# RWKV chunk loop of a two-layer trunk: scores called one stage earlier in the program, and score, mask and state tiles laid out for both directions or both heads at once

## The chip, the cores and the metric

One core of one Trainium2 chip runs the whole kernel. The metric is device microseconds (us) of one execution. Matrix products run on TensorE (PE in the profile; its weight loads are PEld), elementwise work on VectorE (DVE), ScalarE (ACT) and GpSimd (POOL), and DMAs are issued mostly by SyncE (SP).

## The reference, cut to what matters

The model is a trunk of two layers over 256 context and 1024 latent tokens. Each layer mixes tokens by three groups of heads and then runs a mixture of experts. The change concerns the first group, the RWKV-7 mixer: four heads of 64 channels, run over the 1280 tokens forward and backward.

```
def _rwkv7_step(state, inp):
    r, w, k, v, kk, a = inp
    sk = jnp.einsum('dbhvk,dbhk->dbhv', state, kk)
    state = state * w[..., None, :] - sk[..., :, None] * (kk * a)[..., None, :] + v[..., :, None] * k[..., None, :]
    return state, jnp.einsum('dbhvk,dbhk->dbhv', state, r)

def _rwkv7_mixer(za, za_c, lp, with_ctx):
...
    xs = (shared('r'), per_dir('w'), per_dir('k'), shared('v'), shared('kk'), per_dir('a'))
    s0 = jnp.zeros((2, Bn, A_HEADS, HEAD_DIM, HEAD_DIM), F32)
    _, ys = lax.scan(_rwkv7_step, s0, xs)
...
```

Here d is the direction, h the head. The decay w, the key k and the gate a differ by direction; r, v and kk are shared.

## The kernel before, in words

The scan is not run token by token. `rwkv` walks through ten stages of 128 tokens in each direction; a stage holds two chunks of 64 tokens (c), for two directions (d), two pairs of heads (hp) and two heads in a pair (e, one on partitions 0 to 63, the other on 64 to 127). So a stage has 16 units of 64 tokens. Per stage there are four parts.

- `front` (L719 to L790) loads r, k, kk and the low-rank activations, multiplies them out on PE (pu, L735), takes tanh, a running sum (cum, L746) and exponentials, and builds two sets of operands: L1 (kk and r times decays, L776 and L777, one head by DVE and the other by POOL) and bk (b and k times inverse decays, L784 and L785). bw is bk times the decay of the chunk.
- The scores (L798 to L844) turn bw round on PE (pb, L809) into L2 (L812, by ACT), and multiply bk with L1 (pa, L824, each product 128 rows of output: the wanted blocks and others). DVE masks pieces of the result into L1 (L829), Ly (L831) and low (L833); low of direction 0 has products of its own (pf, L840, masked at L841). L1, L2 and Ly are the matrices that the state is multiplied with; low is the strictly lower triangular matrix of a unit.
- The inverse of one plus low: low goes to DRAM and comes back with a 16 by 16 block on each partition (lan, then al). DVE inverts the blocks (`inv16`: L950, then 14 pairs L955 and L956, then L957), and they go back through DRAM into z16 and zt16 (tiles named z). Three products of 16 units and three DVE operations join them to blocks of 32 (`mm8`, L853, called at L857 to L859: pe, pzt, pz), two more sets join those to 64 (L864 and L873, with ACT in between). The result is tt.
- The chain (L889 to L940), two steps in each stage, one per chunk: px (L904) multiplies the state X with L1, ACT copies it (xy, L906), pu2 (L912) multiplies with tt, ACT and DVE write the negated result into X (L913 and L914), pm (L924 and L926) multiplies with Ly and L2, and DVE adds the parts: the new state nx (L930) and the output ys (L935), which a DMA stores per stage (L940). `new_pvu` (L708) makes the tile of the next state and has ACT copy the values v into it (L713). The next step's px needs nx, so the 20 steps of a layer are a chain.

Between these parts `more()` takes the next piece of `in_BC`, the input projection of the other heads: long runs of 16-bit products on PE (L528 to L530, L539 to L541), which depend on nothing in this loop.

The order of every engine's instructions is not the program's. A scheduler sets it when the kernel is built: of the instructions whose inputs its own timeline has ready, it takes the one that stands first in the program, and each engine then works through its queue in that order, waiting where a semaphore is not there yet. Tiles with a tag share `bufs` buffers, and PSUM tiles here come from pools of one to three banks (ps and psc two, psi one); an instruction that needs a buffer waits for its last reader. The first product of the loop starts 229 us into the span in layer 0 and 1997 us in layer 1.

## Time and profile before

| what | value |
|---|---|
| three runs, median (lowest to highest) | 3551.89 us (3545.98 to 3552.17) |
| profiled execution, its own time | 3544.36 us |
| span of the profiled execution | 3541.6 us |
| PE busy in the span | 2930.6 us (83%) |
| DVE busy | 2285.5 us (65%) |
| ACT busy | 1544.1 us (44%) |
| POOL busy | 1007.7 us (28%) |

The span is the time from the first to the last instruction; the execution takes 2.8 us more. Busy time of PE includes products that overlap in the array, so its share says how seldom PE stood still, not how well it was used. A wait is put down to the instruction that released it last. The names of buffers are given without their numbers: L stands for L1 and L2, z for z16 and zt16, pe for the first product of `mm8` and for the one at L864, pu for L735 and pu2 both.

### The profile page before, as it was taken

The page shows a single profiled execution, that of the slowest core. Times are in us where ns is not written, and L with a number is a line of the kernel's source. Part 1 is how long each engine was busy: PE and PEld are TensorE (multiplying, and loading weights), DVE is VectorE, ACT ScalarE, POOL GpSimd, SP SyncE. Part 2 cuts the span into 40 slices and gives each one's busy share as a digit, 9 for nine tenths or more (in the row PEclk, how much of TensorE's full clock was granted, in tenths as well). Part 3 has the DMA queues.
Part 4 walks back from the last instruction along what each step waited for, and adds up shares of the span by engine and source line. Part 5 has one row for each costly group of instructions (what it writes and reads, how often), then busy time and mean ns, then how long its engine had stood idle before and what let it go on. Part 6 is the DMA issues. An engine that isn't in the chain of part 4 may idle for free. (4 is left out here: it accounts for less than half of the span.)

```text
span 3541.6 us, 71217 instructions
## 1 busy us (share of the span) xinstructions
PE 2930.6 (83%) x28620; PEld 1833.0 (52%) x28620; DVE 2285.5 (65%) x4614; ACT 1544.1 (44%) x2769; POOL 1007.7 (28%) x998
## 2 busy tenths in 40 slices
PE   7998889989998788888737998898889866778864
PEld 4656567666755444443325565666666443334431
DVE  4356877368769454557678677783776845554775
ACT  4342444345643154456544434443565314343651
POOL 1122453134424211111165225331433321101113
PEclk9998889999999899999858988899899978888987
DMA  9764343282355789999862542433732769899995
GB/s 375 297 194 111 80 104 89 70 237 71 113 176 199 278 315 384 385 379 367 334 227 78 158 106 77 105 103 95 200 107 73 258 235 363 338 393 364 349 347 198
DMA packets 425468, 773.11 MB, mean 218 GB/s; under 512 B 211152, under 2 KB 340848, under 8 KB 394160
## 3 DMA queue, kind: packets, MB, share of 16 engines
q1 hardware_dynamic: 388048, 697.84, 56.7%
q0 software_dynamic: 36368, 68.07, 5.7%
q8 instruction: 227, 3.72, 0.4%
q10 hardware_dynamic: 720, 2.62, 0.3%
q14 instruction: 105, 0.86, 0.1%
HBM read 653.31 MB, written 114.97 MB: 217 GB/s over the span
## 5 line engine op out<-in xcount | busy, mean ns | idle before, releaser
L1664 PE MATMUL pgate<-wgp,hT 128*32 128x256 f16 (+2 forms) x1704 | 353.1, 376 | 101.8 <-ACT wgp L1613 60.8
L1664 PEld LDWEIGHTS <-hT 128*32 128x32 f16 (+2 forms) x3408 | 206.7, 108 | 334.0 <-issue 172.7
L529 PE MATMUL acc<-hL,wH 128*128 128x256 f16 (+2 forms) x1040 | 346.4, 334 | 13.4 <-POOL hL L486 13.4
L528 PE MATMUL acc<-hH,wH 128*128 128x256 f16 (+2 forms) x1040 | 345.6, 335 | 7.6 <-DVE hH L485 6.6
L530 PE MATMUL acc<-hH,wL 128*128 128x256 f16 (+2 forms) x1040 | 345.4, 333 | 0.0
L1704 PE MATMUL pd<-wdp,gT 128*32 128x256 f16 (+2 forms) x1704 | 221.1, 369 | 37.6 <-DVE gT L1691 21.6
L1195 POOL TENSOR_SCALAR s<-s,rd 128x640 f32<-128x640 f32 (+2 forms) x216 | 171.6, 794 | 222.3 <-DVE rd L1191 97.4
L1622 POOL DMA_INDIRECT xg<-hmoe,map x69 | 87.7, 1271 | 508.4 <-PE ptx L1628 454.5
L1664 PE MATMUL pgate<-wup,hT 128*32 128x256 f16 (+1 forms) x1224 | 196.9, 347 | 19.8 <-DVE wup L1614 12.7
L1614 DVE SCALAR_TENSOR_TENSOR wgp<-wg,wgp 128x2048 f16<-128x2048 f32 x74 | 166.4, 2287 | 63.2 <-ACT wgp L1613 63.1
L1614 DVE SCALAR_TENSOR_TENSOR wdp<-wd,wdp 128x2048 f16<-128x2048 f32 x74 | 166.5, 2287 | 46.9 <-ACT wdp L1613 46.9
L1184 ACT ACTIVATE s<-s,nm 128x640 f32<-128x640 f32 (+2 forms) x216 | 164.4, 763 | 66.1 <-DVE nm L1181 48.6
L1614 DVE SCALAR_TENSOR_TENSOR wup<-wu,wup 128x2048 f16<-128x2048 f32 x74 | 166.3, 2286 | 30.0 <-ACT wup L1613 27.7
L1208 PE MATMUL po<-pt,vt 128*64 128x128 f32 x1920 | 166.9, 288 | 20.2 <-DVE pt L1199 11.7
L1293 PE MATMUL acco<-wo,o 128*128 128x512 f16 x756 | 177.2, 388 | 0.0
L1704 PEld LDWEIGHTS <-gT 128*32 128x32 f16 (+2 forms) x1704 | 97.0, 108 | 147.4 <-DVE gT L1691 30.0
L1613 ACT ACTIVATE wdp<-wd 128x2048 f16<-128x2048 f32 x74 | 137.2, 1903 | 51.0 <-DMA wd<-w_down 44.1
L1717 POOL DMA_DIRECT2D ys<-y x66 | 51.7, 784 | 378.5 <-DVE y L1711 206.9
L1613 ACT ACTIVATE wup<-wu 128x2048 f16<-128x2048 f32 x74 | 137.3, 1903 | 48.7 <-DMA wu<-w_up 48.7
L1613 ACT ACTIVATE wgp<-wg 128x2048 f16<-128x2048 f32 x74 | 137.4, 1902 | 46.0 <-DMA wg<-w_gate 42.7
L1165 PE MATMUL pss<-k,qs 128*128 128x256 f16 (+1 forms) x552 | 127.5, 269 | 31.9 <-DVE mx L1178 18.4
L1672 ACT ACTIVATE sg<-pgate 64x512 f32<-64x512 f32 (+2 forms) x86 | 42.8, 498 | 251.9 <-PE pgate L1664 251.9
(420 smaller groups left out, 7424.2 us busy)
## 6 DMA issues: line engine op xcount, KB each, us to landing
wu<-w_up SPq DMA_DIRECT2D x64, 2048.0 KB
wd<-w_down SPq DMA_DIRECT2D x64, 2048.0 KB
wg<-w_gate SPq DMA_DIRECT2D x64, 2048.0 KB
wmod<-w_mod SPq DMA_DIRECT2D x48, 1024.0 KB
w<-w_in SPq DMA_DIRECT2D x41, 512.0 KB
ld<-ys SPq DMA_DIRECT2D x40, 384.0 KB
z<-inv SPq DMA_DIRECT2D x80, 128.0 KB
ys<-y POOLq DMA_DIRECT2D x20, 512.0 KB
```

The source lines that it names most:

```text
L528: self.nc.tensor.matmul(ov, H[:, k, :], hh, start=k == 0, stop=False)
L529: self.nc.tensor.matmul(ov, H[:, k, :], hl, start=False, stop=False)
L530: self.nc.tensor.matmul(ov, Lo[:, k, :], hh, start=False, stop=k == KD - 1)
L1165: te.matmul(pss[:, o:o + n], qs[:, e, Q], k1[:, e, k0:k0 + n], start=True, stop=False)
L1184: a.activation(s2[:, e, :nk], s2[:, e, :nk], AF.Exp, bias=nm[:, e:e + 1], scale=1.0 / SS, accum_out=den[:, e:e + 1])
L1195: g.tensor_scalar(s2[:, e, :nk], s2[:, e, :nk], rd[:, e:e + 1], SC_Q, OP.mult, OP.mult)
L1208: te.matmul(po[64 * e:64 * e + 64, 0:P], vt[:, kb, 64 * e:64 * e + 64], pt[:, e, x * P:x * P + P], start=x == 0, stop=x == len(kbs) - 1)
L1293: te.matmul(acc, o[:, zo, k] if k < KD - 1 else self.og_last[:, zo, tok], wo[:, zw, k, c], start=k == 0 and y == 0, stop=k == KD - 1 and y ...
L1613: nc.scalar.mul(t[:, 0, c], w[:, c], SC_W)
L1614: nc.vector.scalar_tensor_tensor(t[:, 1, c], w[:, c], SC_W, t[:, 0, c], OP.mult, OP.subtract)
L1664: te.matmul(p[off + i * m:off + i * m + m, :n], part(hT, zh)[:, k, o:o + m], part(w, zw)[:, k, i * n:i * n + n], start=k == 0 and y == 0, ...
L1704: te.matmul(t, part(gT, zh)[:, k, :m], part(wd, zw)[:, k, i * n:i * n + n], start=k == 0 and y == 0, stop=k == 3 and y == len(parts) - 1)
```

## The change

In the program's text the stage is taken apart: a new function `scores(st, ahead)` holds the scores and `inv16`, and it is called for stage st+1 before the joining of the blocks and the chain of stage st; `front` is called for stage st+2 there. Around this, tiles get another order of their dimensions so that one instruction covers what several did:

- L1's operands are made by four DVE operations (one per head and operand, both directions and all chunks) in place of four on DVE and four on POOL.
- The product of all 128 rows (pa) becomes three sets of 64 by 64 blocks: pk (the other head's rows, 128 columns), pr and pf for both directions. DVE masks four pk pieces, one pr and one pf per stage, where it had four, four, and three.
- The running sum takes both pairs of heads at once, `new_pvu` both directions, the copy to L2 both directions, and ys is one operation per step, stored per step.
- `mm8` leaves out the columns that are zero or unchanged: 32 columns in place of 64, and a standing tile E4 with zeros takes the place of E.
- b and k keep the places that they have in bk.

The core of the diff:

```
+            nc.sync.dma_start(vt[st][:, :, 0], self.vst[:, 2 * FSEG[st]:2 * FSEG[st] + 2])
+            for s in range(2):
+                nc.sync.dma_start(vt[st][:, s, 1], self.vst[:, 2 * BSEG[st] + 1 - s])
...
             for d in range(2):
-                for hp in range(2):
-                    v.tensor_tensor_scan(cum[:, d, hp], k2("scan"), th[:, d, hp], 0.0, OP.mult, OP.add)
+                v.tensor_tensor_scan(cum[:, d].rearrange("p h t -> p (h t)"), k2("scan"), th[:, d].rearrange("p h t -> p (h t)"), 0.0, OP.mult, OP.add)
...
-            for d in range(2):
-                for e in range(2):
-                    eng = v if e == 0 else g
-                    eng.tensor_tensor(L1v[hom[e], d, :, e, e], chv(kk_)[hom[e], d], chv(ex)[hom[e], d], OP.mult)
-                    eng.tensor_tensor(L1v[hom[e], d, :, e, 1 - e], chv(r_)[hom[e], d], chv(cum)[hom[e], d], OP.mult)
...
+            for e in range(2):
+                o = hom[e]
+                for i, (x, y) in enumerate(((kk_, ex), (r_, cum))):
+                    v.tensor_tensor(L1p[o, :, :, e, i], pieces(x)[o], pieces(y)[o], OP.mult)
...
+        def scores(st, ahead):
             L1, bk, bw, wt, seg = ahead
-            if st < 9:
-                ahead = front(st + 1)
-            more()
...
-                            te.matmul(pas[e][:, i * 128:i * 128 + 128], bk[hom[e], d, hp, c].rearrange("p s t -> p (s t)"),
-                                      L1[hom[e], d, c, hp, e].rearrange("p s t -> p (s t)"), start=True, stop=True)
...
+                            te.matmul(pk[hom[1 - e], 2 * hp + c], bk[hom[e], d, hp, c, 1 - e, :],
+                                      L1[hom[e], d, hp, c, e].rearrange("p s t -> p (s t)"), start=True, stop=True)
+                for e in range(2):
+                    o = hom[1 - e]
+                    v.tensor_tensor(L1[o, d, :, :, e].rearrange("p h c s t -> p (h c) (s t)"), pk[o],
+                                    k2(f"mL1_{d}")[o].unsqueeze(1).to_broadcast([64, 4, 128]), OP.mult)
...
+                            te.matmul(pr[hom[e], i], b_, r1, start=True, stop=True)
+
+                            x, y = (K_, b_) if d == 0 else (b_, K_)
+                            te.matmul(pf[hom[e], i], x, y, start=True, stop=True)
+            v.tensor_tensor(Ly.rearrange("p d h c t -> p d (h c) t"), pr.rearrange("p (d u) t -> p d u t", d=2),
+                            k2("mR").rearrange("p (d t) -> p d t", d=2).unsqueeze(2).to_broadcast([P, 2, 4, 64]), OP.mult)
+            v.tensor_tensor(low.rearrange("p d h c t -> p (d h c) t"), pf, k2("mLow").unsqueeze(1).to_broadcast([P, 8, 64]), OP.mult)
...
             z16, zt16 = self.inv16(rp, st % 2)
+            return L1, L2, Ly, lowu, z16, zt16, wt, seg
+
+        ahead = front(0)
+        made = scores(0, ahead)
+        ahead = front(1)
+        for st in range(10):
+            L1, L2, Ly, lowu, z16, zt16, wt, seg = made
+            if st < 9:
+                made = scores(st + 1, ahead)
+            if st < 8:
+                ahead = front(st + 2)
+            more()
...
-            E = rp.tile([P, 8, 64], F32, tag="E", name="E", bufs=1)
-            v.tensor_tensor(E, mm8("pe4", lowu, zt16), k2("mE4").unsqueeze(1).to_broadcast([P, 8, 64]), OP.mult)
-            v.tensor_tensor(zt16, zt16, mm8("pzt", z16, E), OP.subtract)
-            v.tensor_tensor(z16, z16, mm8("pz", E, z16), OP.subtract)
...
+            lo16, up16 = halves(z16)[:, :, :, 0], halves(zt16)[:, :, :, 1]
+            Eh = halves(E4)[:, :, :, 1]
+            v.tensor_tensor(Eh, mm8("pe4", lowu, up16), k2("mE4").rearrange("p (g t) -> p g t", t=16).unsqueeze(1).to_broadcast([P, 8, 2, 16]), OP.mult)
+            pzt = mm8("pzt", z16, Eh)
+            v.tensor_tensor(up16, up16, pzt, OP.subtract)
+            v.tensor_tensor(lo16, lo16, mm8("pz", E4, lo16), OP.subtract)
...
-                for e in range(2):
-                    o = hom[1 - e]
-                    for d in range(2):
-                        c = s if d == 0 else 1 - s
-                        v.tensor_tensor(ys[o, d, c], pm[o, 1, d], xy[o, d, :, e, :], OP.add)
+                ys = rp.tile([P, 2, 2, 64], F32, tag="ys", name="ys", bufs=2)
+                v.tensor_tensor(ys, pm[:, 1], xy[:, 1], OP.add)
+                for d in range(2):
+                    nc.sync.dma_start(y_d[d, 2 * seg[d] + cs[d]], ys[:, d])
```

The scheduler makes another order of it. Three places follow; the line numbers in the rows of the changed kernel are its own.

**PE, layer 0, around the first step of a chain.** In the kernel before, at a place where px of one stage stands (L904, its operand is L_3014):

```order
L904 MATMUL px<-pvu,L_3014 64x64 x16
L853 MATMUL pe_4361<-z_1_4357,low 64x64 x16
L840 MATMUL pf<-bk,L_4167 64x64 x6
L912 MATMUL pu_4033<-xy,z_1_3847 64x64 x4
L912 MATMUL pu_4033<-xy,z_0_3843 64x64 x4
L840 MATMUL pf<-bk,L_4167 64x64 x2
```

In the changed kernel, where px has the operand L_2172 (L924 is px, L931 pu2, L871 `mm8`, L822 pk, L836 pr, L839 pf):

```order
L944 MATMUL pmy<-pvu,L_2185 64x64 x8
L942 MATMUL pmy<-pvu,Ly 64x64 x8
L822 MATMUL pk<-L_3425,bk 64x128 x16
L871 MATMUL pe_4045<-z_1_3375,low 64x32 x7
L924 MATMUL px<-pvu,L_2172 64x64
L871 MATMUL pe_4045<-z_1_3375,low 64x32
L924 MATMUL px<-pvu,L_2172 64x64 x15
L871 MATMUL pe_4045<-z_1_3375,low 64x32 x2
L836 MATMUL pr<-L_3425,bk 64x64 x15
L839 MATMUL pf<-bk,L_3425 64x64 x5
L931 MATMUL pu_3723<-xy,z_1_2306 64x64 x4
L931 MATMUL pu_3723<-xy,z_0_2302 64x64 x4
```

In both, the first product of the next stage's joining (pe) and the scores of the stage after it (L_4167, L_3425) stand around px of the chain's stage; what moved is that pk, pr and pf now follow one another in that place, where pa stood in pieces among other work.

**DVE, layer 0, around the start of an inverse.** Before (L914 writes X, L930 the next state, L950 starts the inverse):

```order
L829 TENSOR_TENSOR L_3657<-pa,c_1919 64x2x2x128
L831 TENSOR_TENSOR Ly<-pa,c_1919 64x2x2x64
L833 TENSOR_TENSOR low<-pa,c_1919 64x256
L914 TENSOR_SCALAR pvu<-pu_3534 64x2x2x64
L841 TENSOR_TENSOR low<-pf,c_1919 128x256
L930 TENSOR_TENSOR pvu<-pmy,xw 64x2x2x64 x2
L935 TENSOR_TENSOR ys<-pmy,xy 64x128 x4
L950 TENSOR_TENSOR zl<-c_1919,al 64x256
```

In the changed kernel (L933 writes X, L948 the next state, L876 and L878 belong to `mm8`, L965 starts the inverse):

```order
L826 TENSOR_TENSOR L_2356<-pk,c_1919 64x4x128 x4
L933 TENSOR_SCALAR pvu<-pu_3048 64x4x64
L840 TENSOR_TENSOR Ly<-pr,c_1919 128x512
L842 TENSOR_TENSOR low<-pf,c_1919 128x512
L876 TENSOR_TENSOR E_1939<-pe_3543,c_1919 128x16x16
L1085 TENSOR_TENSOR xp<-prope,rope 128x512
L948 TENSOR_TENSOR pvu<-pmy,xw 64x4x64 x2
L950 TENSOR_TENSOR ys<-pmy,xy 128x256
L965 TENSOR_TENSOR zl<-c_1919,al 64x256
L970 TENSOR_TENSOR il<-al,zl 64x14
L971 TENSOR_TENSOR zl<-zl,il 64x14
L878 TENSOR_TENSOR z_1_2306<-z_1_2306,pzt 128x16x16
```

The operation that finishes the joined block zt16 (L878) now stands behind the start of the next stage's inverse.

**DVE, layer 0, around the end of an inverse.** Before, at the end of one inverse (L957 is its last operation):

```order
L955 TENSOR_TENSOR il<-al,zl 64x26
L914 TENSOR_SCALAR pvu<-pu_3972 64x2x2x64
L956 TENSOR_TENSOR zl<-zl,il 64x2x13
L955 TENSOR_TENSOR il<-al,zl 64x14
L956 TENSOR_TENSOR zl<-zl,il 64x14
L957 COPY zl<-zl 64x256
```

In the changed kernel (L972 is the last operation of the inverse):

```order
L970 TENSOR_TENSOR il<-al,zl 64x26
L971 TENSOR_TENSOR zl<-zl,il 64x2x13
L970 TENSOR_TENSOR il<-al,zl 64x14
L971 TENSOR_TENSOR zl<-zl,il 64x14
L972 COPY zl<-zl 64x256
L933 TENSOR_SCALAR pvu<-pu_3664 64x4x64
L506 SCALAR_TENSOR_TENSOR wL<-w,wH 128x1024
L948 TENSOR_TENSOR pvu<-pmy,xw 64x4x64 x2
```

The operation that writes X for the first step of the stage (L933) moved from among the inverse's last operations to behind them.

## Rows read from the trace of the kernel before

**Rows 1.** Stretches by engine: us, busy per engine, granted clock, DMA share and GB/s.

```profile
core 0: us, PE busy (x) PEld busy (x) DVE busy (x) ACT busy (x) POOL busy (x), PEclk, DMA share, GB/s
...
348.00:704.00 356.00, 315.33 (x4571) 226.20 (x4568) 240.00 (x595) 140.12 (x360) 131.47 (x129) 0.90 0.34 88
400.00:500.00 100.00, 87.24 (x1114) 59.50 (x1113) 77.79 (x173) 41.81 (x108) 53.30 (x49) 0.85 0.37 95
500.00:600.00 100.00, 87.42 (x1311) 66.43 (x1309) 79.28 (x206) 43.45 (x116) 40.69 (x39) 0.93 0.38 94
...
2113.00:2462.00 349.00, 315.63 (x4653) 229.02 (x4652) 240.68 (x594) 140.83 (x359) 129.80 (x124) 0.92 0.34 87
```

**Rows 2.** DVE's X product, both layers: form, count | busy, mean ns | idle before, releaser.

```profile
L914 DVE TENSOR_SCALAR pvu<-pu 64x256 f32<-64x256 f32 x40 | 17.1, 427 | 67.1 <-ACT pvu L913 66.5
```

**Rows 3.** DVE in layer 0, start us and us: from low to the inverse.

```profile
529.42 0.42 DVE L841 TENSOR_TENSOR low<-pf,c 128x256 f32<-128x256 f32 x1
531.82 0.87 DVE L930 TENSOR_TENSOR pvu<-pmy,xw 64x256 f32<-64x256 f32 x2 [1.98 <-PE pmy L924]
532.62 0.99 DVE L935 TENSOR_TENSOR ys<-pmy,xy 64x128 f32<-64x128 f32 x4
...
537.38 0.42 DVE L950 TENSOR_TENSOR zl<-c,al 64x256 f32<-64x256 f32 x1 [3.18 <-issue]
```

**Rows 4.** SP in the same stretch: the load of the blocks.

```profile
534.16 0.59 SPq L947 DMA_DIRECT2D al<-lan  x1
```

**Rows 5.** DVE groups of both layers, by form, as in rows 2.

```profile
L829 DVE TENSOR_TENSOR L<-pa,c 64x512 f32<-64x512 f32 x80 | 54.8, 684 | 11.1 <-PE pa L824 10.2
L784 DVE SCALAR_TENSOR_TENSOR bk<-th,wv 64x512 f32<-64x512 f32 x40 | 46.1, 1152 | 1.3 <-ACT wv L756 0.7
L777 DVE TENSOR_TENSOR L<-ld,cum 64x256 f32<-64x256 f32 x40 | 42.5, 1095 | 0.2
L935 DVE TENSOR_TENSOR ys<-pmy,xy 64x128 f32<-64x128 f32 x160 | 39.0, 283 | 8.0 <-PE pmy L924 7.5
L776 DVE TENSOR_TENSOR L<-ld,ex 64x256 f32<-64x256 f32 x40 | 35.4, 918 | 0.7 <-ACT ex L757 0.5
L746 DVE TENSOR_TENSOR_SCAN cum<-c,th 128x128 f32<-128x128 f32 x80 | 34.9, 485 | 0.6
L831 DVE TENSOR_TENSOR Ly<-pa,c 64x256 f32<-64x256 f32 x80 | 33.8, 422 | 1.2
L833 DVE TENSOR_TENSOR low<-pa,c 64x256 f32<-64x256 f32 x40 | 16.6, 414 | 1.4 <-PE pe L864 1.3
L857 DVE TENSOR_TENSOR E<-pe,c 128x512 f32<-128x512 f32 x20 | 13.7, 685 | 9.1 <-PE pe L853 8.7
L955 DVE TENSOR_TENSOR il<-al,zl 64x56 f32<-64x56 f32 x40 | 10.7, 267 | 1.1
L841 DVE TENSOR_TENSOR low<-pf,c 128x256 f32<-128x256 f32 x20 | 8.4, 420 | 10.6 <-PE pf L840 10.2
```

**Rows 6.** PE groups of both layers, by form.

```profile
L824 PE MATMUL pa<-L,bk 64*128 64x128 f32 x640 | 80.5, 310 | 12.0 <-DVE zl L956 5.2 <-DVE Ly L831 4.2 <-ACT L L812 2.4
L853 PE MATMUL pe<-z,low 64*64 64x64 f32 x640 | 32.4, 243 | 22.5 <-DMA z<-inv 22.5
```

**Rows 7.** PE in layer 1: runs of like products, start us, us of the run, rows.

```profile
2383.02 0.32 PE L875 MATMUL p<-z,E 32*32 32x32 f32 x10
2383.28 1.16 PE L824 MATMUL pa<-L,bk 64*128 64x128 f32 x8
...
2384.92 0.93 PE L824 MATMUL pa<-L,bk 64*128 64x128 f32 x6
...
2418.93 0.38 PE L529 MATMUL acc<-hL,wH 128*128 128x512 f16 x1
2419.24 0.33 PE L853 MATMUL pe<-z,low 64*64 64x64 f32 x2
2419.49 0.39 PE L530 MATMUL acc<-hH,wL 128*128 128x512 f16 x1
2419.81 0.92 PE L853 MATMUL pe<-z,low 64*64 64x64 f32 x24
...
2420.92 0.33 PE L853 MATMUL pe<-z,low 64*64 64x64 f32 x4
```

More of the change, by code (lines that the diff above doesn't have):

```diff
@@ L790, in front @@
             return L1, bk, bw, wt, seg
-        ahead = front(0)
-        for st in range(10):
+        def scores(st, ahead):
             L1, bk, bw, wt, seg = ahead
-            if st < 9:
-                ahead = front(st + 1)
-            more()
             low = rp.tile([P, 2, 2, 2, 64], F32, tag="low", name="low", bufs=2)
@@ L810, in rwkv @@
             for e, pb in enumerate(pbs):
[L811 to L815 removed]
+                a.copy(L2[:, :, :, :, e].rearrange("p d h c t -> p (d h c) t"), pb.rearrange("p (u t) -> p u t", t=64))
             for d in range(2):
[L819 removed]
+                pk = ps.tile([P, 4, 128], F32, tag=tag, name="pk")
@@ L835, in rwkv @@
-            pf = ps.tile([P, 512], F32, tag=tag, name="pf")
-            for hp in range(2):
-                for c in range(2):
-                    for e in range(2):
-                        i = 2 * hp + c
-                        te.matmul(pf[hom[e], i * 64:i * 64 + 64], L1[hom[e], 0, c, hp, e, e, :], bk[hom[e], 0, hp, c, e, :], start=True, stop=True)
-            v.tensor_tensor(low[:, 0], pf[:, 0:256].rearrange("p (h c t) -> p h c t", h=2, c=2), mask("mLow", slice(0, 128), 64), OP.mult)
+                            te.matmul(pk[hom[1 - e], 2 * hp + c], bk[hom[e], d, hp, c, 1 - e, :],
+                                      L1[hom[e], d, hp, c, e].rearrange("p s t -> p (s t)"), start=True, stop=True)
@@ L938, in rwkv @@
             more()
-            for d in range(2):
-                nc.sync.dma_start(y_d[d, 2 * seg[d]:2 * seg[d] + 2].rearrange("c p h t -> p c h t"), ys[:, d])
     def inv16(self, rp, b):
```

89 lines of the change are left out of this document (42 added, 47 removed).

## The prediction

> **What bounds the kernel now.** I first read the stretches by engine [rows 1]. The loop runs from 348 to 704 us in layer 0 (ten stages, 35.6 us each) and from 2113 to 2462 in layer 1 (34.9 each). No engine is full: DVE is busy for 240 us of 356, PE for 315. But in the middle stages (400 to 600) PE stands at 87% and DVE at 78 to 79%, at a granted clock of 0.85 to 0.93. Two engines near full, each waiting for the other in turn, is what the reader should see.
>
> Next, the groups by line, to find where the chain waits. DVE is idle for 67.1 us before the X product (L914), and 66.5 of these end with ACT's half of the same pair [rows 2]: ACT had waited for pu2, and pu2 for tt. So the chain is late because the inverse's tail is late, in the first of a stage's two steps. The inverse is late for a reason that DVE's timeline shows: low is finished at 529.84, but the inversion begins at 537.38, 7.5 us later [rows 3]. In between DVE does chain work (nx 0.87, ys 0.99) and waits 3.18 us; SP issues the load of the blocks at 534.16 [rows 4], so the way through DRAM is what it waits for. The ring is: L1's operands, scores and masks on DVE, DRAM, 28 small operations of DVE, DRAM, joining on PE and DVE, X, the next state. Most of its links are on DVE, in one queue.
>
> **Look-ahead.** By the text the scores come one stage earlier. By the order of the queues they hardly do: in both kernels, while the chain of a stage runs, the next stage is being joined and the one after is scored (the operands in the rows of PE's order). I cost this part at zero; the change is worth the work that it takes off DVE and PE.
>
> **DVE, both layers (20 stages)** [rows 5].
> Removed: L776 35.4 and L777 42.5, the scan 34.9, Ly 33.8, low 16.6 and 8.4, three operations of `mm8` per stage (60 at 0.685, as E, 41.1), ys 39.0. Together 251.7.
> Added:
> - 80 operations for L1 of 64x512, without a row of their own. The nearest of this size are the pa mask with one input in PSUM (0.684) and bk with both in SBUF (1.152). I take the middle, 0.92: 73.6 (54.7 to 92.2).
> - 40 scans of 256 elements: 0.485 for 128, so at most 0.97; by the slope between 256 and 512 elements elsewhere (0.422 and 0.684, 1.02 ns each) 0.62. I take 0.75: 30 (24.6 to 38.8).
> - Ly and low over all 128 partitions at 0.684, 20 each: 27.4.
> - 60 operations of `mm8` with 256 elements at 0.42 (as L841): 25.2. 40 ys at 0.42: 16.8.
> Together 173.0, a saving of 79 us (51 to 103), 3.95 per stage. The four pk masks per stage have the size of the four pa masks: no change.
>
> The rows speak for the dear end of the first price: L777, both inputs in SBUF and POOL at work beside it, takes 1.095 for half of that size, where L831 with an input in PSUM takes 0.422. The Trainium skill (SBUF — State Buffer, section "Who interferes with whom") says that DVE's second pair of ports is shared with GpSimd as an exclusive lock; by it the new operations would be slow wherever POOL works beside them, and the saving would be some 60, an estimate. The trace agrees that these forms are slow; POOL itself loses its half of L776 and L777, so the lock would be held less.
>
> **PE, both layers.** pa is 640 rows in the trace; two more rows in a run cost 1.16 − 0.93 = 0.23, so 0.115 each [rows 7]: 73.6. pk has as many, each of 64 by 128, and its two heads sit in opposite quarters of the array. Products of 64 columns that sit so (L853) cost (0.92 − 0.33)/20 = 0.0295 a row [rows 7] (two to 24 rows of one line); for 128 columns that is 0.059: 37.8. If they don't overlap, 73.6. pf's 320 rows become 1280 of pr and pf: 960 more at 0.0295, +28.3. `mm8`'s 1920 rows go from 0.0295 to between that and half of it, I take 0.017: −24. The order has about 100 fewer changes between kinds of product, at some 0.1 each (a lone pair takes 0.33 [rows 7], against 0.06 in a run): −10. Net −41.5, from −51 to about 0, or 2.1 per stage.
>
> The order puts pk's two heads into one bank of PSUM. L853 does the same with its two halves, and 24 rows still take 0.92 us [rows 7], so I count the overlap. The Trainium skill (TensorEngine Tiling (Array Packing), section "Gotcha 1: PSUM Pressure") says that different row tiles cannot access the same bank at once; by it pk would keep 0.115 a row and PE would save about 6 us, an estimate. The trace here disagrees for L853's products.
>
> **At nothing.** ACT issues fewer copies (v, L2) and POOL loses its half of the operands; neither is waited for with more than a few us. SP gets three more DMAs per stage (v and y), 0.59 each as the row of SP has it [rows 4], 1.8 us per stage; the cover is that SP's queue has no work of its own, and if it went, al's issue would be late by that. The input projection left over behind the chain gets 48 products of 512 columns shorter in layer 0 and 48 longer in layer 1, at 0.38 [rows 7] 18 us each way: zero.
>
> **The sum.** I take DVE's saving as the stage's, for its queue holds most of the ring; PE's (31.5 a stage less 2.1, in a stage of 31.3 to 31.6) is then covered by it, and becomes next in line. The last two stages of each layer make no new front or inverse, so 16 stages count: 16 × 3.95 = −63 us. The profiled execution took 3544.4 (span 3541.6 and 2.8 around it), the runs' median is 7.5 above. On the median's scale: 3552 − 63 = **3489**; by DVE's ends (51 and 103, eight tenths of each) 3470 to 3511. What is late next is PE.
>
> **Rivals.**
> 1. PE alone sets the time: only PE's saving counts and its idle time stays. For it: PE's 87% in the middle [rows 1]. Against: the 67 us [rows 2] are a wait for the ring, not for PE's queue. 3552 − 41 = 3511.
> 2. Both count, and the wait of the first joining product for z's landing (22.5 us [rows 6]) goes, because the inverse is done earlier. −63 − 41 − 22 = 3425. For it: the order has the inverse's end well ahead of pe. Against: PE can't be more than full.
> 3. Slower: head-of-line waits on DVE. In the new order the inversion's start (L965) stands before L878, and the X product of the first step (L933) behind the whole inverse. Between low and L965 there is now less chain work (0.42 and 0.87 and 0.42, 1.7 us), so of the 7.5 us up to 5.8 are a wait instead of 3.2: +2.6. And X may have to let 22 operations of the inverse at 0.267 and four L1 operands at 0.92 pass, 9.6 us, against some 26 products of PE at 0.243 [rows 6] (6.3) that lie before pm anyway: +3.3. Less the 3.95 saved: +1.9 × 16 = +31, 3583. It decides from the point at which PE reaches pm before DVE has ended the inverse. For it: the order. Against: the scheduler's timeline thought all of these ready by then, and SP's issue of al comes soon after low.
> 4. The change does not do what it says: look-ahead was there, and DVE's freed time becomes a longer wait for al (3.18 of 7.5 already is [rows 3]). 3552.
>
> **How the numbers follow.** The forecast gets 0.41: it rests on the one wait that is long and on rows for most of its terms. PE alone 0.17, both 0.14, slower 0.18, nothing 0.10. Faster by over 0.2% (7 us, about what a measurement of this kernel can tell from no change) is 0.41 + 0.17 + 0.14 = 0.72; same 0.10; slower 0.18. The range leaves out half of rival 2 below 3425 and most of rival 3 above 3560: 3425 to 3560. The forecast's own range is 3470 to 3511.
>
> **What would show it.** In the changed profile: stages of about 31.3 us; the L1 operands (L790) at 0.7 to 1.15, Ly and low (L840, L842) near 0.68, ys (L950) at 0.42; DVE busy about 40 us less in each layer; the 67 us before the X product (now L933) down to a third. For PE: a run of pk at 0.06 a row; at 0.115 the overlap failed. For rival 3: idle time before L965 above 3.2 a stage, and idle PE before pm released by DVE's X. For rival 4: stages of 35 us with DVE idle more. The prediction is wrong if DVE's work falls as counted and the stage stays above 34 us, or if PE's busy share in the middle stages goes to 95% with DVE idle.

## The result, and the profile after

The change made the kernel slower: 3596.97 us (median of four runs, 3591.78 to 3600.37) against 3548.93 for the kernel before on the same chip, a ratio of 1.0138 with a 95% interval of 1.0114 to 1.0162. The forecast was 3489, with a range from 3425 to 3560. The profiled execution has a span of 3592.3 us, 50.7 more than before.

Where it went. In layer 0 nothing was lost: the last state of the chain comes at 707 us (688 before), but the products of the input projection that are left over behind the chain end at 730 (734 before). In layer 1 the last state comes at 2482 (2453), and the left-over products end at 2525 (2467), so 58 us are lost there. The stretches show why; they are the changed kernel's, by engine, with the columns of [rows 1]:

```profile
348.00:704.00 356.00, 309.60 (x4867) 230.49 (x4866) 225.44 (x493) 131.76 (x312) 109.79 (x97) 0.91 0.35 87
2113.00:2462.00 349.00, 278.77 (x4248) 205.99 (x4246) 224.46 (x478) 119.44 (x278) 104.24 (x89) 0.84 0.33 82
2462.00:2520.00 58.00, 58.00 (x854) 43.30 (x850) 15.57 (x37) 18.60 (x42) 10.25 (x12) 1.00 0.43 115
```

In layer 1's loop PE is busy for 278.8 us where it was for 315.6 [rows 1]; the 37 us stand behind the loop, where PE works for 58 us without a gap and DVE for 15.6. No engine got more work: over the whole span DVE's busy time fell from 2285.5 to 2242.1 us, PE's from 2930.6 to 2924.1 and POOL's from 1007.7 to 939.0. The stages became longer because they wait.

TensorE's granted clock does not order the times. It is a mean of stretches at the two levels of 1.2 and 2.4 GHz, as a share of the higher one. In layer 1's loop it fell from 0.92 to 0.84, but in layer 0's it stayed (0.90 and 0.91), and the stages grew in both. Of two kernels that come later in the text, `front_first` has shorter stages than the changed kernel at 0.86 and 0.85 (360 to 680 and 2120 to 2430 us), and `whole_inverse` has stages as long at 0.89 and 0.93.

The groups of DVE by form, both layers, that answer to [rows 2] and [rows 5] (busy, mean ns of one, idle before and releaser):

```profile
L790 DVE TENSOR_TENSOR L<-ld,cum 64x512 f32<-64x512 f32 x40 | 59.3, 1483 | 0.6
L826 DVE TENSOR_TENSOR L<-pk,c 64x512 f32<-64x512 f32 x80 | 55.1, 689 | 17.9 <-PE pk L822 16.5
L790 DVE TENSOR_TENSOR L<-ld,ex 64x512 f32<-64x512 f32 x40 | 45.1, 1129 | 0.3
L749 DVE TENSOR_TENSOR_SCAN cum<-c,th 128x256 f32<-128x256 f32 x40 | 25.8, 685 | 0.2
L933 DVE TENSOR_SCALAR pvu<-pu 64x256 f32<-64x256 f32 x40 | 17.1, 428 | 77.1 <-ACT pvu L932 76.6
L950 DVE TENSOR_TENSOR ys<-pmy,xy 128x256 f32<-128x256 f32 x40 | 17.0, 425 | 4.1 <-PE pmy L942 2.9
L840 DVE TENSOR_TENSOR Ly<-pr,c 128x512 f32<-128x512 f32 x20 | 13.8, 689 | 32.0 <-PE pr L836 27.7 <-PE pf L839 4.2
L842 DVE TENSOR_TENSOR low<-pf,c 128x512 f32<-128x512 f32 x20 | 13.6, 681 | 3.3 <-PE pf L839 3.3
L965 DVE TENSOR_TENSOR zl<-c,al 64x256 f32<-64x256 f32 x20 | 9.9, 493 | 49.2 <-DMA al<-lan 36.7 <-issue 12.5
L876 DVE TENSOR_TENSOR E<-pe,c 128x256 f32<-128x256 f32 x20 | 8.3, 417 | 1.6 <-PE pe L871 1.5
```

The reader is to see two things. Most sizes are as forecast (scan 0.685, ys 0.425, Ly and low 0.69 and 0.68, E 0.42); only L1's operands are dearer. And the wait of 67.1 us ahead of the X product, which was to fall to a third, rose to 77.1.

What became long is the inverse. DVE's timeline in layer 0, from the first operation of an inverse (L965) to its last (L972):

```profile
410.59 0.42 DVE L965 TENSOR_TENSOR zl<-c,al 64x256 f32<-64x256 f32 x1 [4.37 <-DMA al<-lan]
411.04 0.17 DVE L970 TENSOR_TENSOR il<-al,zl 64x14 f32<-64x14 f32 x1
...
412.20 1.27 DVE L749 TENSOR_TENSOR_SCAN cum<-c,th 128x256 f32<-128x256 f32 x2
...
415.85 1.38 DVE L784 SCALAR_TENSOR_TENSOR bk<-th,wv 64x512 f32<-64x512 f32 x2
417.26 0.20 DVE L970 TENSOR_TENSOR il<-al,zl 64x50 f32<-64x50 f32 x1
417.38 2.36 DVE L790 TENSOR_TENSOR L<-ld,ex 64x512 f32<-64x512 f32 x2
419.75 2.73 DVE L790 TENSOR_TENSOR L<-ld,cum 64x512 f32<-64x512 f32 x2
422.52 1.16 DVE L971 TENSOR_TENSOR zl<-zl,il 64x50 f32<-64x50 f32 x1
423.71 1.94 DVE L970 TENSOR_TENSOR il<-al,zl 64x54 f32<-64x54 f32 x1
...
432.02 0.37 DVE L972 COPY zl<-zl 64x256 f32<-64x256 f32 x1
```

And one of the kernel before, of the same layer:

```profile
458.22 0.42 DVE L950 TENSOR_TENSOR zl<-c,al 64x256 f32<-64x256 f32 x1 [0.44 <-DMA al<-lan]
...
467.62 0.37 DVE L957 COPY zl<-zl 64x256 f32<-64x256 f32 x1
```

The first takes 21.8 us, the second 9.8. In the first the front of the stage after next stands inside the inverse: scan, bk and all of L1's operands. In DVE's queue of the changed kernel bk and L1's operands stand inside all 18 inverses that have a front to come; before, 6 of 20 had operands of L1 inside. The two examples are far apart for that reason, and the means are closer: before, the 6 inverses with L1's operands inside took 26.2 us on average and the 14 others 11.6; in the changed kernel the 18 took 22.0 and the 2 others 8.9.

The table follows that through every kernel of this study; `less_pe` and `front_less_pe` leave out work, as said below. It is worked out from the start and end times in one profiled execution of each kernel: the inverse from its first to its last operation (mean of 20); pu2's wait for tt in a stage's first step (from the end of xy to pu2's start); how long after pu2's end DVE's half of X (ACT's in the three kernels with `chain_off` in their names) starts in the first and second step; and the time from one stage's last state to the next's (means of stages 1 to 8, both layers; in the last column layer 0 / layer 1). The kernel before took 3549 to 3555 us on the chips where the others were measured, so differences of a few us between rows say nothing.

| kernel | us | ratio to before (95%) | inverse | wait for tt | X after pu2 | stage |
|---|---|---|---|---|---|---|
| before | 3549 to 3555 | | 16.0 | 8.2 | 1.1, 5.4 | 36.8 / 36.2 |
| changed | 3597.0 | 1.0138 (1.0114 to 1.0162) | 20.7 | 13.2 | 1.6, 1.1 | 40.3 / 42.2 |
| old_layout_new_loop | 3659.7 | 1.0303 (1.0274 to 1.0332) | 21.1 | 15.4 | 5.0, 1.1 | 47.8 / 47.1 |
| old_loop | 3577.1 | 1.0087 (1.0061 to 1.0113) | 13.9 | 9.7 | 4.7, 4.3 | 40.3 / 44.2 |
| front_first | 3541.3 | 0.9969 (0.9946 to 0.9992) | 15.2 | 7.9 | 0.8, 5.9 | 38.5 / 36.2 |
| old_layout_front_first | 3543.9 | 0.9981 (0.9957 to 1.0005) | 17.8 | 5.8 | 1.1, 6.0 | 37.1 / 35.4 |
| whole_inverse | 3578.6 | 1.0089 (1.0051 to 1.0126) | 10.9 | 7.6 | 5.7, 2.1 | 40.5 / 42.2 |
| pool_half | 3631.0 | 1.0240 (1.0204 to 1.0276) | 20.8 | 13.8 | 2.3, 2.0 | 43.0 / 43.4 |
| low_first | 3563.8 | 1.0041 (1.0022 to 1.0061) | 16.4 | 11.3 | 1.9, 5.7 | 42.6 / 42.2 |
| front_low_first | 3595.1 | 1.0136 (1.0099 to 1.0174) | 20.1 | 8.7 | 3.4, 6.2 | 45.1 / 38.3 |
| old_loop_low_first | 3583.7 | 1.0088 (1.0060 to 1.0117) | 12.2 | 11.8 | 2.1, 2.0 | 44.0 / 42.5 |
| join_first | 3680.4 | 1.0345 (1.0310 to 1.0381) | 21.2 | 2.7 | 10.1, 1.3 | 46.6 / 46.3 |
| join_low_first | 3572.6 | 1.0052 (1.0034 to 1.0070) | 13.9 | 5.1 | 3.1, 1.3 | 42.8 / 40.9 |
| join_front_first | 3613.3 | 1.0169 (1.0138 to 1.0200) | 14.4 | 4.5 | 3.8, 3.7 | 40.4 / 38.5 |
| old_layout_join_first | 3651.1 | 1.0282 (1.0242 to 1.0321) | 21.5 | 12.8 | 6.0, 1.8 | 46.6 / 44.8 |
| chain_off | 3567.1 | 1.0039 (1.0016 to 1.0062) | 20.7 | 13.6 | 0.5, 0.5 | 41.0 / 39.5 |
| join_chain_off | 3674.7 | 1.0346 (1.0296 to 1.0397) | 20.5 | 3.3 | 6.0, 0.5 | 45.1 / 45.9 |
| front_chain_off | 3539.3 | 0.9960 (0.9937 to 0.9983) | 13.0 | 9.5 | 0.6, 0.8 | 37.6 / 35.4 |
| less_pe | 3541.0 | 0.9963 (0.9944 to 0.9981) | 21.7 | 11.1 | 1.8, 3.6 | 41.4 / 40.8 |
| front_less_pe | 3488.8 | 0.9812 (0.9774 to 0.9851) | 15.4 | 4.8 | 1.2, 6.7 | 35.4 / 34.0 |

From before to changed, pu2's wait grew by 5.0 us a stage and the inverse by 4.7. The X product of the second step came 4.3 sooner. The rest of the two steps took about 4 us more, most of it between X and the next state (1.0 in the first step, 2.2 in the second). A stage is 4.7 us longer in the end.

The table also shows that a short inverse is not enough: `old_loop`, `old_loop_low_first` and `whole_inverse` have inverses of 11 to 14 us and times of 3577 to 3584.

### The profile page after: what moved, and what is told of

It is laid out like the page before. It is cut to its first block, busy times and chain, and to the rows that moved or that the text cites. A ratio compares the mean times of both kernels' runs of the same rounds, so it can differ in the third digit from the quotient of the medians.

```text
span 3592.3 us, 72718 instructions
## 1 busy us (share of the span) xinstructions
PE 2924.1 (81%) x29580; PEld 1839.5 (51%) x29580; DVE 2242.1 (62%) x4354; ACT 1523.6 (42%) x2649; POOL 939.0 (26%) x920
## 5 line engine op out<-in xcount | busy, mean ns | idle before, releaser
L528 PE MATMUL acc<-hH,wH 128*128 128x256 f16 (+2 forms) x1040 | 345.2, 335 | 10.9 <-DVE hH L485 9.5
L1679 PE MATMUL pgate<-wup,hT 128*32 128x256 f16 (+1 forms) x1224 | 195.8, 349 | 18.4 <-DVE wup L1629 15.4
L1687 ACT ACTIVATE sg<-pgate 64x512 f32<-64x512 f32 (+2 forms) x86 | 42.8, 498 | 272.9 <-PE pgate L1679 272.7
## 6 DMA issues: line engine op xcount, KB each, us to landing
ys<-y POOLq DMA_DIRECT2D x20, 512.0 KB, 11.1
```

Source lines behind the costliest of these rows:

```text
L528: self.nc.tensor.matmul(ov, H[:, k, :], hh, start=k == 0, stop=False)
L1679: te.matmul(p[off + i * m:off + i * m + m, :n], part(hT, zh)[:, k, o:o + m], part(w, zw)[:, k, i * n:i * n + n], start=k == 0 and y == 0, ...
```

## The experiments

**Loop or layouts?** Theory A: the loop's new order costs the time. Theory B: the new layouts do. `old_loop` keeps all layouts and puts the old loop back; `old_layout_new_loop` is the reverse.

```
         ahead = front(0)
-        made = scores(0, ahead)
-        ahead = front(1)
         for st in range(10):
-            L1, L2, Ly, lowu, z16, zt16, wt, seg = made
+            now = ahead
             if st < 9:
-                made = scores(st + 1, ahead)
-            if st < 8:
-                ahead = front(st + 2)
+                ahead = front(st + 1)
             more()
+            L1, L2, Ly, lowu, z16, zt16, wt, seg = scores(st, now)
```

> The changed kernel with all its new layouts, but the loop of the kernel before (front of the next stage, then scores, inverse, joining and chain of this stage). In the changed kernel the inverse takes about 21 us from its first to its last operation, and 10 to 12 before. Theory A, the loop's order: with the new order of calls the next front's bk, L1, scan and exponent operations stand inside the inverse's 28 dependent operations in DVE's queue; here they mostly don't, so the inverse falls to some 12 us, a stage is 3 to 5 us shorter than in the changed kernel, and the time is near the forecast, 3470 to 3520. Rival B, the layouts: L1's new operations at 1.1 to 1.5 us and the PE blocks cost the time wherever they stand; then the time stays within 15 us of the changed kernel's 3597. Rival C, nothing of either alone: 3552.

> The kernel before with its old layouts and only the new loop (scores and inverse of the next stage, then the front of the one after, ahead of the joining and the chain). Theory A: this alone makes the kernel slower, and by more than the whole change, for the layouts' saving is not there: 3620 to 3680, the inverse at 20 us or more. Rival B (the layouts cost the time): 3540 to 3560. Rival C (only both together are slow): 3552.

Measured 3577.1 and 3659.7. With the old layouts the new loop costs 109 us, in theory A's range. `old_loop` falls in none of its ranges: the layouts in the old loop don't gain 63 us, they lose 27, though the inverse is short there (13.9). (The 10 to 12 us that I gave there for the inverse before fit only those without L1's operands inside; the mean is 16.0.) pk starts 34 and 45 us after the last write of its operands in the two layers (stages 1 to 8; 21 and 20 for pa before): the scheduler put the scores later there; why is open.

**The front's place alone.** `front_first` calls `front(st + 2)` ahead of `scores(st + 1)` (and ahead of the loop `front(1)` ahead of `scores(0)`), nothing else.

```
         ahead = front(0)
+        nxt = front(1)
         made = scores(0, ahead)
-        ahead = front(1)
         for st in range(10):
             L1, L2, Ly, lowu, z16, zt16, wt, seg = made
+            ahead = nxt
+            if st < 8:
+                nxt = front(st + 2)
             if st < 9:
                 made = scores(st + 1, ahead)
-            if st < 8:
-                ahead = front(st + 2)
             more()
```

> The changed kernel, with the front of stage st+2 called ahead of the scores of st+1, and nothing else moved: the joining and the chain are still called last. Theory A in its narrow form (the front's operations inside the inverse are the cost): the inverse falls to 12 to 14 us and the time to 3480 to 3530. Theory A in its wide form (joining and chain come last in the program, so everything else goes ahead of them in every queue): the time stays above 3560, though the inverse is shorter. Rival B: 3597 within 15.

Measured 3541.3, 56 us below the changed kernel and 0.3% below the kernel before (0.9946 to 0.9992). An inverse of layer 1:

```profile
2174.38 0.42 DVE L966 TENSOR_TENSOR zl<-c,al 64x256 f32<-64x256 f32 x1 [5.39 <-DMA al<-lan]
...
2177.17 0.87 DVE L949 TENSOR_TENSOR pvu<-pmy,xw 64x256 f32<-64x256 f32 x2
...
2184.98 0.37 DVE L973 COPY zl<-zl 64x256 f32<-64x256 f32 x1
```

It takes 11.0 us, with the scan and the chain's next state inside but no L1 operand. In 5 of the 20 inverses L1's operands still stand inside, and the mean is 15.2. Over both layers the wait ahead of the X product is 57.9 us (77.1 in the changed kernel):

```profile
L934 DVE TENSOR_SCALAR pvu<-pu 64x256 f32<-64x256 f32 x40 | 17.1, 428 | 57.9 <-ACT pvu L933 57.1
```

The time missed the narrow form's upper end by 11 us, and the inverse its 12 to 14; the wide form, that joining and chain as the last calls are the cost, fell. Stages 1 to 8 of both layers together take 62 us less than in the changed kernel. Against the kernel before they gain nothing (38.5 and 36.2 us a stage, 36.8 and 36.2 before), and the first product behind layer 1's attention (acco) starts at 2726 us, 6 later than before: that the span is 3 us shorter than before comes from work behind it, which the change does not touch.

**Is low on a ring?** `low_first` moves pf, low and its DMA to the head of `scores` (the lines of pf, the mask and the two stores are put ahead of `pbs`); `front_low_first` and `old_loop_low_first` do so on the two kernels above. `pool_half` gives two of L1's four operations to POOL:

```
-                    v.tensor_tensor(L1p[o, :, :, e, i], pieces(x)[o], pieces(y)[o], OP.mult)
+                    (v if e == 0 else g).tensor_tensor(L1p[o, :, :, e, i], pieces(x)[o], pieces(y)[o], OP.mult)
```

> The changed kernel with one edit in the scores: the products pf, the mask to low and low's DMA are called first, ahead of pb, pk and pr (they need none of these). In the changed kernel low of stage k+2 comes behind the joining product pe of stage k+1 in PE's queue, and pe waits for the blocks to land; so inverse (22 us), DRAM (5), low (8 to 9) and DRAM (7) follow each other, 43 us from one inverse to the next in layer 1. Theory A with this ring: low leaves the ring, an inverse follows the last one by 34 to 38 us, the time falls by 60 to 130 us, to 3470 to 3540. If only the front's operations inside the inverse matter: the masks of pk take their place inside the inverse (62 of them stand there in DVE's queue), the inverse stays at 18 us or more and the time at 3560 to 3600. Theory B (the layouts cost the time): 3597.

> Both edits: the front called ahead of the scores (that run took 3541) and pf, low and its DMA first in the scores. If ring and inverse add up: below 3520, stages under 35 us. If the front's place alone was the cure: 3541 within 10. If PE (85% busy in its loop) has become the bound: no more than 10 us below 3541.

> The new layouts, the old loop and pf, low and its DMA first in the scores. The new layouts in the old loop took 3577, 27 more than before, with DVE waiting 37 and 42 us per layer part for the load of al. If low's late place in the program (behind pk and pr, where before the last piece of pa gave half of it) is the reason, the wait for al shrinks and the time comes to 3490 to 3540. If the old loop with the new layouts is slow for another reason (the chain waits for the joining, which starts when the chain before it ends): 3565 to 3585.

> The changed kernel with one half of L1's operand products (two of four per stage) on POOL, as before the change. DVE's queue keeps its order: the front's bk and the other two stand inside the inverse as in the changed kernel. Theory A: 2 x 1.3 us leave the inverse in each of 16 to 18 stages, which is 42 to 47 us if the inverse lies on the ring, less what POOL's work costs the inverse's small operations by standing beside them (0.2 us alone, 1.1 to 1.9 beside POOL): 3555 to 3590. Theory B (L1 on DVE is slow by itself, and DVE's busy time counts): the same 42 us or more, 3540 to 3555. If neither the inverse nor DVE sets the stage: 3597 within 10.

Measured 3563.8, 3595.1, 3583.7 and 3631.0. In `low_first` the blocks land 24 to 27 us before the joining starts, and tt is still late (pu2 waits 11.3 us): low is not the ring. The 33 us gained do not stand in the stages either, which are no shorter than in the changed kernel (42.6 and 42.2 us): the first stage of each layer ends 25 and 27 us earlier. Put on `front_first` the same edit loses 54, outside all its ranges: such edits don't add up. `old_loop_low_first` is no better than `old_loop`, as its second range said; no inverse has L1's operands inside there, and tt is late all the same (11.8). `pool_half` fell outside all its cases, and on the slow side: two operations left the inverse, but its own 30 small operations grew from 9.6 to 11.9 us an inverse, so that it stayed at 20.8.

**Is the joining late because it is called late?** In `join_first` the block of `scores(st + 1)` and `front(st + 2)` moves behind the joining of st (behind the line that makes tt), ahead of its chain; `join_low_first` has pf and low first as well, `join_front_first` front before scores, `old_layout_join_first` the old layouts.

> The changed kernel with the joining of stage st (mm8, pe, p, tt) called ahead of the scores of st+1 and the front of st+2, and the chain of st behind them as it was. In the changed kernel tt is ready 17 us after the chain before it has ended (8 to 10 before the change), and from pe to tt it takes 29 to 35 us (26 before). With pf first this wait stayed at 15 to 16 us although the blocks had landed 24 to 27 us before the joining began: so the joining, not the inverse, was late there. Theory J (the joining stands behind the scores and the front of later stages in the program and so in the queues): pe to tt falls to 20 us or less, tt comes 5 to 10 us after the chain before it, and the time is 3500 to 3550. Theory A alone (the front's operations inside the inverse, which stay there): the inverse stays at 20 us or more, tt late by 15 and the time 3580 to 3600.

> The joining first and also pf, low and its DMA first in the scores, so that the blocks land long before the joining. If inverse and joining each cost their part (A and J): better than join_first by 20 us or more, 3460 to 3520. If the chain of px, pu2 and pm with its own waits, or PE, is the bound by then: within 10 us of join_first.

> Order of calls: joining of st, front of st+2, scores of st+1, chain of st. Against front_first (3541) only the joining moves ahead, against join_first only the front. A and J together: inverse near 14 us and tt 5 to 8 us after the chain before it, 3480 to 3530. If the joining's place does nothing: 3541 within 10.

> The old layouts in the same order of calls as join_first. The old layouts in the new loop took 3660. What is left between this and join_first is the worth of the layouts in one and the same order: by the forecast of their work on DVE (3.95 us a stage on 16 stages) 63 us; by the two runs in the new loop, 3660 and 3597, also 63. If their saving is only had where DVE is the ring, and the joining's wait is the bound: under 25.

Measured 3680.4, 3572.6, 3613.3 and 3651.1. In `join_first` the joining did what theory J said (19 us from pe to tt, pu2 waits 2.7), and the time, which theory J put at 3500 to 3550, rose by 83 us: DVE's half of X now came 10.1 us after pu2, behind the long inverse. This is rival 3 of the prediction, not in the changed kernel but in this one. `join_low_first` is better than `join_first` by 108 us, more than the 20 expected, but 53 above its range; `join_front_first` has the short inverse that was expected (14.4) and a short wait for tt (4.5), and is 83 above its range and 72 slower than `front_first`. The layouts in this order are a loss of 29 us, where a gain of 63 or of under 25 was expected.

**Is it the chain's own place in DVE's queue?** `chain_off`, `join_chain_off` and `front_chain_off` take the chain off DVE; PE gets eight more products of 64 columns per step.

```
-                v.tensor_scalar_mul(X[64:128, 1, :, :, 1, :], pu2[64:128], -1.0)
+                a.mul(X[64:128, 1, :, :, 1, :], pu2[64:128], -1.0)
...
-                                    te.matmul(pm[hom[e], 0, d, hp, :], L2[:, d, hp, cs[d], e, :], U, start=True, stop=True)
+                                    te.matmul(pm[hom[e], 0, d, hp, :], L2[:, d, hp, cs[d], e, :], U, start=True, stop=False)
+                                    te.matmul(pm[hom[e], 0, d, hp, :], self.ident[:, hom[e]], xw[:, d, hp, :], start=False, stop=True)
...
-                        v.tensor_tensor(nx[hom[e], 0, :, :, e, :], pm[hom[e], 0], xw[hom[e]], OP.add)
+                        a.copy(nx[hom[e], 0, :, :, e, :], pm[hom[e], 0])
```

> The changed kernel with the chain's elementwise work taken off DVE: ACT writes both halves of X, PE adds the decayed state (an identity product onto pm) and ACT copies pm to the next state. In the changed kernel pu2 of the first step waits 13.2 us for tt, and DVE's half of X comes only 1.6 and 1.1 us after pu2, so what DVE's queue costs the chain directly is small. Theory T (the inverse, stretched by the front's operations, makes tt late): at most 25 us gained, 3570 to 3600, pu2's wait as long as before. Rival Q (the chain's own operations stand in DVE's queue behind the inverse, rival 3 of the prediction): 3500 to 3550.

> The same edit on join_first (3680), where pu2 waits only 2.7 us for tt but DVE's half of X comes 10.1 us after pu2, behind the inverse. If the inverse, one block of 21 us in DVE's queue, is what the chain lets pass once per stage, either ahead of tt or ahead of X: with X and the next state off DVE nothing of it is left, 9 us less on 16 stages, 146 us, so 3520 to 3560. If the joining's own DVE operations (E, zt16, z16) then stand behind the inverse instead: 3590 to 3680.

> The same edit on front_first (3541), where DVE's half of X comes 0.8 us after pu2 in the first step and 5.9 in the second, and pu2 waits 7.9 us for tt. 5 us less on 16 stages would be 80 us: 3455 to 3480. If tt is as late as before and its wait takes up what X gives: 3520 to 3545. If PE, with 640 identity rows more and 85% busy, is the bound: 3541 to 3570.

> The old layouts in the order of calls of front_first (the changed kernel's layouts take 3541 there). The layouts' worth was 63 us in the new loop (3660 less 3597), minus 27 in the old loop (3550 less 3577) and minus 29 with the joining first (3651 less 3680). If it follows DVE's saving wherever the inverse is not in the way: 3590 to 3605. If the order of the queues decides and the layouts' work is covered: within 25 us of 3541.

Measured 3567.1, 3674.7, 3539.3 and 3543.9. `chain_off` gained 30 us, 5 more than theory T allowed, and kept its wait for tt (13.6): rival Q, with 3500 to 3550, fell. In `front_chain_off` the 5.1 us per stage that X had waited are gone, and the time is the same within 2 us. pu2 waits 1.6 more, and px of a stage's first step starts 3.5 us after the state that it needs (0.3 in `front_first`), with joining products and the projection ahead of it on PE: something else holds the stage at 36 to 37. `join_chain_off` stayed slow, as its second case said, so DVE's place behind the inverse was not all of it; X comes 6 us after pu2 there though ACT writes it. And in `front_first`'s order the layouts are worth 3 us, which is within the spread between chips.

**The inverse alone, and PE.** `whole_inverse` keeps the changed kernel's calls and only queues the front behind the last operation of the inverse on DVE. `less_pe` and `front_less_pe` leave out the third product (low half of the weights) of the input projection in `in_BC`.

```
             if st < 8:
-                ahead = front(st + 2)
+                with self.tc.issue_after(self.inv_end):
+                    ahead = front(st + 2)
...
-        v.tensor_copy(zl[:, 1], Z.rearrange("p r c -> p c r"))
+        self.inv_end = v.tensor_copy(zl[:, 1], Z.rearrange("p r c -> p c r")).ins
```

```
-            self.nc.tensor.matmul(ov, Lo[:, k, :], hh, start=False, stop=k == KD - 1)
+            if low:
+                self.nc.tensor.matmul(ov, Lo[:, k, :], hh, start=False, stop=k == KD - 1)
...
-            self.nc.tensor.matmul(o, hh, Lo[:, k, :], start=False, stop=k == KD - 1)
...
```

> The changed kernel and its order of calls, with one thing forced in DVE's queue: the operations of front(st+2) are queued behind the last operation of the inverse of st+1, so none of them stands inside it. Nothing is left out. Theory T: the inverse falls from 20.7 to 12 to 14 us, pu2's wait for tt from 13.2 to about 8, and the time to 3520 to 3565. If the front, now later, makes scores and the next inverse late by as much (one ring of DVE work, in whatever order): pu2 waits 12 us or more and the time is 3590 to 3680, as with the joining called first.

> The changed kernel with one of the three 16-bit products of the other heads' input projection left out (low half of the weights): a third of the projection's PE time, by its rows some 150 us in the two loops together. In the changed kernel's layer 1 PE is busy for 79% of the loop and the stages are set by the late tt: then stages stay at 38 to 42 us, and what is gained is the projection's rest behind the chain (some 40 us in layer 1, 15 in layer 0) and its part outside the loops: 3500 to 3550. If PE sets the stage after all: 3430 to 3470.

> The same left out of front_first (3541), where PE is busy for 85 to 89% of the loop. If PE's work is what bounds the kernels with a good order (which would say why the layouts, that take work from DVE but none from PE, are worth 3 us there): stages of 37 us fall to 31 to 33, and the time to 3400 to 3440. If the wait for tt is a ring of its own there too: stages stay above 35 and the time at 3480 to 3520.

Measured 3578.6, 3541.0 and 3488.8. `whole_inverse` did to tt what theory T said (the inverse 10.9 us, pu2's wait 7.6), but its time lies between the two ranges, 18 us below the changed kernel. An inverse of it, and what follows:

```profile
455.62 0.42 DVE L966 TENSOR_TENSOR zl<-c,al 64x256 f32<-64x256 f32 x1 [5.96 <-issue]
...
462.79 0.37 DVE L973 COPY zl<-zl 64x256 f32<-64x256 f32 x1
...
463.98 1.27 DVE L749 TENSOR_TENSOR_SCAN cum<-c,th 128x256 f32<-128x256 f32 x2
...
468.66 1.54 DVE L790 TENSOR_TENSOR L<-ld,ex 64x512 f32<-64x512 f32 x1
```

The inverse takes 7.5 us, but the next front, and with it pk and low, comes behind it: low of the next stage is ready 23 us after the blocks of this one have landed (9 in the changed kernel), and X of the first step starts 5.7 us after pu2. The stage is as long as ever (40.5 and 42.2 us), and the last states come 12 and 9 us later than in the changed kernel. So the 18 us are not tt's: PE does more of the projection inside layer 1's loop, and the left-over products end at 2485, 6 us before the last state, in place of 2525. The inverse's length makes tt late, but it is one link; that the order of inverse, front and masks on DVE decides as a whole is what these runs suggest, and no run shows it by itself.

With a third of the projection's products gone, the changed kernel's stages stayed at 41 us, so PE does not bound it, as the first case said; what was gained is the rest behind the chain, which ended at 2431, ahead of the last state (2451), in place of 2525. `front_first` fell from 37.4 to 34.7 a stage, between the two cases expected: PE (85 to 89% busy there) is part of its bound, but not all.

## Why the prediction was wrong

**The step that failed is in the paragraph "Look-ahead": "I cost this part at zero".** I compared how many stages ahead the scores stand and found no difference; I did not ask what the new order of calls puts inside the inverse (only rival 3 lets X pass four operations of L1). There the front of a later stage had come in, in 18 of 20 inverses, and it makes tt late: pu2 waits 13.2 us in place of 8.2, and 7.6 when `whole_inverse` queues the front behind the inverse. What the order of calls costs in time is shown by two runs: `old_layout_new_loop` prices the new loop at 109 us with the old layouts, and `front_first` takes 56 us of the changed kernel's time back by moving the front's call. That the late tt is all of this cost is not shown, for `whole_inverse` has the short wait and stages as long as the changed kernel's. I even showed a piece of that queue, and read in it only where L933 and L878 stood.

**The second failed step is "I take DVE's saving as the stage's".** The 63 us were there in one order (3660 less 3597; that the figure is the forecast's own is luck, for DVE's work fell by less than forecast), were about nothing in `front_first`'s order and a loss of 27 and 29 in two others. DVE is busy for two thirds of a loop: in these four orders its saving came to the time in one only.

**DVE's sum.** The rows of [rows 5] that went are 251.7 us; the new ones are 104.4 for L1 (73.6 forecast, 92.2 the upper bound), 25.8 for the scans, 27.4, 24.7 and 17.0: 199.3, a saving of 52, at the lower bound of 51. The term that was mis-sized is L1's, which lies above its own upper bound. bk fell by 14.8 besides, and the inverse's small operations rose from 148.2 to 174.6. DVE's busy time fell by 43 us in all. L1's operands, both inputs in SBUF, take 1.13 and 1.48 on average where 0.69 does with an input in PSUM. The form itself is not slow: 15 of the 80 had POOL at work for less than half of their time, and these took 0.67 to 0.69; the 65 others took 1.45 on average. The Trainium skill (SBUF — State Buffer, "Who interferes with whom") says that DVE shares its second pair of ports with GpSimd and that this pair is an exclusive lock; the trace agrees, by these figures.

**PE's sum.** PE's busy time fell by 6.5 us and not 41.5. (The 0.0295 a row in the forecast is the slope from the run of four rows, which takes 0.33 too; from two rows, as the text has it, it is 0.027.) pk is near its price: 26 rows in 1.64 us are 0.063 each at most, 0.059 was forecast, and its two heads do overlap in one bank:

```profile
2149.03 1.64 PE L822 MATMUL pk<-L,bk 64*64 64x128 f32 x26
```

Over both layers pa's 80.5 us became pk's 44.8, as forecast. `mm8`, half as wide, costs as much as before; the first row is the changed kernel's, the second the one before's, both at a granted clock of 1.00, the level of 2.4 GHz:

```profile
405.79 1.12 PE L871 MATMUL pzt<-E,z 64*64 64x32 f32 x32
```

```profile
2229.88 1.15 PE L853 MATMUL pzt<-E,z 64*64 64x64 f32 x32
```

So its −24 was nothing: its three groups together are busy for 90.0 us and were for 84.8. pr and pf were mis-sized too. They stand between other products, and in place of 17.0 us for pf before they are busy for 83.6, where +28.3 was forecast:

```profile
L836 PE MATMUL pr<-L,bk 64*64 64x64 f32 x640 | 39.7, 248 | 0.1
L839 PE MATMUL pf<-L,bk 64*64 64x64 f32 x320 | 22.5, 233 | 0.0
L839 PE MATMUL pf<-bk,L 64*64 64x64 f32 x320 | 21.4, 252 | 0.7 <-DVE L L826 0.7
```

**Rivals.** Rival 3 named the side and nearly the time (3583), which was luck, for it did not name the mechanism: the idle time before the inverse's first operation (L950 before, L965 now) rose only from 41.4 to 49.2 us in 20 stages, and X came 1.6 us after pu2.

```profile
L950 DVE TENSOR_TENSOR zl<-c,al 64x256 f32<-64x256 f32 x20 | 8.5, 426 | 41.4 <-DMA al<-lan 26.5 <-DMA ys<-ys 7.5 <-issue 6.7
```

The term for the left-over projection ("zero") holds in sign for each layer, 23 us less behind the chain in layer 0 and 29 more in layer 1, but the layers don't cancel: in layer 0 the rest had hidden the longer chain, in layer 1 it came on top.

**What stays open.** Three things are not shown: what holds the stage at 36 to 37 us in all the better orders (neither PE alone nor the chain's own operations on DVE), why the layouts lose in the old loop, and which link makes the stage long in the orders that have a short inverse.

## What to carry to other kernels

Before counting work removed from an engine, look at what the scheduler puts between the dependent small operations of the longest chain: here a loop order that makes bulk work ready there cost more than the work saved. Test the loop's order and the layouts apart, for their effects don't add. The version to keep of the new layouts is the one with the front called first: 3541 us, 56 below the changed kernel by moving the front's call, and about level with the kernel before (0.3% below, with an interval of 0.1 to 0.5%).

## What the runs showed of the hardware

The small DVE operations of the inverse have both inputs in SBUF. In the changed kernel 484 of the 560 had POOL at work for less than half of their time, and none of these took over 0.21 us. Of the 76 others 57 took over 0.7, up to 1.94, and each of the 57 ends 0.03 to 0.07 us after an operation of POOL does: DVE waits out POOL's operation, however small its own is. (The same holds for all 32 such operations before and all 95 in `pool_half`.) The two at 422.52 and 423.71 above stand beside these of POOL:

```profile
420.23 3.38 POOL L785 TENSOR_TENSOR bk<-kd,wv 64x512 f32<-64x512 f32 x2
423.69 1.89 POOL L793 TENSOR_TENSOR bw<-bk,wt 128x1024 f32<-128x1024 f32 x1
```

The operation at 423.71 ends at 425.65, just after POOL's (425.58). `pool_half`, with more on POOL, has five such operations over 0.7 us in each inverse, the changed kernel three. And in runs of fp32 products with 64 rows of weights, 32 columns take hardly less time than 64 (1.12 and 1.15 us for 32 rows of the trace at a granted clock of 1.00).
